# Im2col on one core: eight channels per partition, loads of growing size, first stores of three planes

## The chip, the core and the metric

The kernel runs on one core of a Trainium2 chip. The metric is the device time in microseconds, the median of several runs. Five engines matter by name: VectorE (DVE in the profile) and ScalarE (ACT) copy data inside SBUF, SyncE (SP) issues the transfers, GpSimd (POOL) and TensorE (PE) do no work here. Sixteen DMA engines move the data between HBM and SBUF.

## The reference

The input `x` has 16 batches of 64 channels of 32x32 float32. For each channel, each of the nine offsets of a 3x3 window gives one plane of 30x30 values, cut from the channel at that offset. The output has 16 x 576 planes of 900 values. It is data movement only: 4.19 MB read, 33.18 MB written, no arithmetic.

```python
cols = np.zeros((batch, c * kernel_size * kernel_size, h_out * w_out), dtype=np.float32)
for b in range(batch):
    col_idx = 0
    for i in range(h_out):
        for j in range(w_out):
            patch = x[b, :, i:i + kernel_size, j:j + kernel_size].copy()
            cols[b, :, col_idx] = patch.ravel()
            col_idx += 1
```

## The kernel before, in words

`_im2col_fast` runs with two channels per partition (`CPP` is 2, the first candidate that fits). The 16 x 64 channels make 512 pairs, which are 4 groups of 128 partitions. All four loads are issued first (L32), on SyncE's queue: each brings 128 rows of 8 KB (two channels), 1 MB in all, into an `in_tile` of its own.

Then, for each group, an `out_tile` of 2 x 9 planes per partition (64,800 bytes) is filled by 18 copies of 128x900. Even copies go to ScalarE (L50), odd ones to VectorE (L52), so each engine gets nine. A copy reads a 30x30 window from rows of 32 and writes 900 values in a row. There are two buffers for `out_tile`: the third group's copies must wait until the first group's stores have landed, and the fourth group's for the second's.

Group 0 is stored in two halves, one channel each (L56, 128 rows of 32,400 bytes); groups 1 to 3 are stored in one transfer each (L62, 128 rows of 64,800 bytes). The output of one group is one contiguous stretch of HBM. All loads and stores are issued by SyncE in the order of the program, on one queue. No order is written by hand beyond that; semaphores follow from the tiles' reads and writes.

Of the kernel before, what the change touches and what calls it, by code (L numbers as in the profile page):

```python
# [1 line left out]

# [4 lines left out]


def _im2col_fast(ctx, tc, x, K, out, CPP):  # L10
    nc = tc.nc
    P = nc.NUM_PARTITIONS

    B, C, H, W = x.shape
    HO = H - K + 1
    WO = W - K + 1
    KK = K * K

    ROWS = B * C // CPP
    n_groups = ROWS // P  # L20

    x_v = x.rearrange("b (cp c2) h w -> (b cp) c2 (h w)", c2=CPP)
    out_v = out.rearrange("b (cp c2 kk) n -> (b cp) c2 (kk n)", c2=CPP, kk=KK)

    in_pool = ctx.enter_context(tc.tile_pool(name="in_pool", bufs=n_groups))
    out_pool = ctx.enter_context(tc.tile_pool(name="out_pool", bufs=2))

    in_tiles = []
    for g in range(n_groups):
        row0 = g * P  # L30
        in_tile = in_pool.tile([P, CPP, H, W], x.dtype, name="in_tile")
        nc.sync.dma_start(  # L32
            out=in_tile,
            in_=x_v[row0 : row0 + P].rearrange("r c2 (h w) -> r c2 h w", h=H),
        )
        in_tiles.append(in_tile)

    for g in range(n_groups):
        row0 = g * P
        in_tile = in_tiles[g]  # L40
        out_tile = out_pool.tile([P, CPP, KK, HO, WO], x.dtype)

        ncopy = 0
        for c2 in range(CPP):
            for kk in range(KK):
                ki, kj = divmod(kk, K)
                src = in_tile[:, c2, ki : ki + HO, kj : kj + WO]
                dst = out_tile[:, c2, kk]
                if ncopy % 2 == 0:
                    nc.scalar.copy(out=dst, in_=src)  # L50
                else:
                    nc.vector.tensor_copy(out=dst, in_=src)  # L52
                ncopy += 1

            if g == 0:
                nc.sync.dma_start(  # L56
                    out=out_v[row0 : row0 + P, c2],
                    in_=out_tile[:, c2].rearrange("p kk i j -> p (kk i j)"),
                )

        if g != 0:
            nc.sync.dma_start(  # L62
                out=out_v[row0 : row0 + P].rearrange("r c2 n -> r (c2 n)"),
                in_=out_tile.rearrange("p c2 kk i j -> p (c2 kk i j)"),
            )


def _im2col_generic(ctx, tc, x, K, out):
    nc = tc.nc
    P = nc.NUM_PARTITIONS  # L70

    B, C, H, W = x.shape
    HO = H - K + 1
    WO = W - K + 1
    KK = K * K

    x_rows = x.rearrange("b c h w -> (b c) (h w)")
    out_rows = out.rearrange("b ck n -> (b ck) n").rearrange(
        "(bc kk) n -> bc (kk n)", kk=KK
    )  # L80

    n_rows = B * C
    n_groups = (n_rows + P - 1) // P

    in_pool = ctx.enter_context(tc.tile_pool(name="in_pool", bufs=min(n_groups, 4)))
    out_pool = ctx.enter_context(tc.tile_pool(name="out_pool", bufs=2))

    for g in range(n_groups):
        row0 = g * P
        nrows = min(P, n_rows - row0)  # L90

        in_tile = in_pool.tile([P, H, W], x.dtype, name="in_tile_g")
        nc.sync.dma_start(
            out=in_tile[:nrows],
            in_=x_rows[row0 : row0 + nrows].rearrange("r (h w) -> r h w", h=H),
        )

        out_tile = out_pool.tile([P, KK, HO, WO], x.dtype, name="out_tile_g")
        for kk in range(KK):
            ki, kj = divmod(kk, K)  # L100
            src = in_tile[:nrows, ki : ki + HO, kj : kj + WO]
            dst = out_tile[:nrows, kk]
            if kk % 2 == 0:
                nc.scalar.copy(out=dst, in_=src)
            else:
                nc.vector.tensor_copy(out=dst, in_=src)

        nc.sync.dma_start(
            out=out_rows[row0 : row0 + nrows],
            in_=out_tile[:nrows].rearrange("p kk i j -> p (kk i j)"),  # L110
        )


@with_exitstack
def kernel(
    ctx: ExitStack,
    tc: tile.TileContext,
    x: bass.AP,
    kernel_size: bass.AP,
    out: bass.AP,  # L120
):
    nc = tc.nc
    P = nc.NUM_PARTITIONS

    K = int(kernel_size)
    B, C, H, W = x.shape
    HO = H - K + 1
    WO = W - K + 1
    KK = K * K
    assert out.shape == (B, C * K * K, HO * WO)  # L130

    dt_size = mybir.dt.size(x.dtype)

    CPP = 0
    for cand in (2, 1):
        if C % cand:
            continue
        rows = B * C // cand
        if rows % P:
            continue  # L140
        free_bytes = cand * KK * HO * WO * dt_size
        if free_bytes >= 2**16:
            continue
        n_groups = rows // P
        sbuf_need = 2 * free_bytes + n_groups * cand * H * W * dt_size
        if sbuf_need > 190 * 1024:
            continue
        CPP = cand
        break

    if CPP:
        _im2col_fast(ctx, tc, x, K, out, CPP)
    else:
        _im2col_generic(ctx, tc, x, K, out)


# [1 line left out]
_INS = ['x', 'kernel_size']  # L158
_OUTS = [((16, 576, 900), 'float32')]
#: Inputs that are plain numbers.  # L160
_NUMBERS = {'kernel_size': 3}


# [26 lines left out]
```

## Time and profile before

| | us |
|---|---|
| median of 3 runs | 92.85 (92.7 to 93.08) |
| span of the profiled execution | 91.3 |
| DVE busy, 36 copies | 19.6 |
| ACT busy, 36 copies and a table load | 32.0 |
| mean of a copy, ACT / DVE | 0.938 / 0.623 |
| first load issued / first copies start | 0.73 / 5.61 |

The span is the time from the first to the last instruction of one profiled execution. The runs are timed apart from it, and their median is 1.5 us above it; the profiled execution has no timed value of its own. Over the span the core moved 37.37 MB, a mean of 409 GB/s. A load took a median of 7.9 us from its issue to its landing, the two half stores 16.6 us, the three full stores 30.5 us.

The profile's slices divide the span into 40 equal pieces; a digit is the busy share in tenths. "DMA" in the tables by stage is the mean busy share of the 16 DMA engines. A packet is one row of a transfer, moved by one of them; the trace has the start, length and size of each packet.

### The profile page before, as it was taken

What the parts mean: (1) busy time and instruction counts of PE and PEld (TensorE: products, weight loads), DVE (VectorE), ACT (ScalarE), POOL (GpSimd) and SP (SyncE); (2) the same over time, 40 slices, a digit from 0 to 9 for tenths busy, and PEclk for the clock granted to TensorE, in tenths of its full rate; (3) what the DMA queues carried; (4) which work ended last, traced back from release to release, by engine and by line L of the source; (5) the groups of instructions that cost most, each with busy time, mean ns of one, the idle gap of its engine ahead of it and who ended that gap; (6) DMA issues with size and microseconds to landing.
All of it is one profiled execution on the core that took longest, in us unless ns stands there. A gap on an engine that the chain in (4) does not pass through costs nothing.

```text
span 91.3 us, 141 instructions
## 1 busy us (share of the span) xinstructions
DVE 19.6 (22%) x36; ACT 32.0 (35%) x37; POOL 0.2 (0%) x4
## 2 busy tenths in 40 slices
DVE  0059997000000049600000199000000000000000
ACT  5059999991000049980000199920000000000000
POOL 0000000000000000000000000000000000000000
DMA  2899999999999999899999999999999999999960
GB/s 36 373 406 431 427 463 426 412 440 440 426 426 440 554 454 398 369 426 398 454 454 454 454 454 454 454 454 454 454 454 426 426 398 398 426 426 426 426 284 0
DMA packets 1297, 37.37 MB, mean 409 GB/s; under 512 B 145, under 2 KB 145, under 8 KB 145
## 3 DMA queue, kind: packets, MB, share of 16 engines
q1 hardware_dynamic: 1296, 37.37, 95.7%
q14 instruction: 1, 0.00, 0.0%
HBM read 4.19 MB, written 33.18 MB: 409 GB/s over the span
## 4 chain that ended last, share of the span: by engine, by line
DMA 40%; ACT 24%; ACTq 1%; issue 0%
DMA out_dram<-out_tile 34%; ACT out_tile L50 24%; DMA in_tile<-in_x_dram 5%; ACTq L185 1%; ACTq L50 0%
## 5 line engine op out<-in xcount | busy, mean ns | idle before, releaser
L50 ACT COPY out_tile<-in_tile 128x900 f32<-128x900 f32 x36 | 30.7, 938 | 27.2 <-DMA out_dram<-out_tile 23.6
L52 DVE COPY out_tile<-in_tile 128x900 f32<-128x900 f32 x36 | 19.6, 623 | 37.6 <-DMA out_dram<-out_tile 31.9
L50 ACT ACT_TABLE_LOAD x1 | 1.3, 1283 | 0.7 <-PEq L171 0.7
L171 POOL MEMSET const-bfloat16-1.0<- 128x1 bf16 x1 | 0.1, 102 | 0.0
L171 POOL MEMSET const-uint8-127<- 128x1 uint8 x1 | 0.1, 102 | 0.0
L171 POOL MEMSET const-float32-0.0<- 128x1 f32 x1 | 0.1, 99 | 0.2 <-issue 0.2
L171 POOL MEMSET const-float32-1.0<- 128x1 f32 x1 | 0.1, 99 | 0.0
## 6 DMA issues: line engine op xcount, KB each, us to landing
out_dram<-out_tile SPq DMA_DIRECT2D x3, 8100.0 KB, 30.5
out_dram<-out_tile SPq DMA_DIRECT2D x2, 4050.0 KB, 16.6
in_tile<-in_x_dram SPq DMA_DIRECT2D x4, 1024.0 KB, 7.9
```

Source lines behind the costliest of these rows:

```text
L50: nc.scalar.copy(out=dst, in_=src)
L52: nc.vector.tensor_copy(out=dst, in_=src)
L171: nc = _bacc.Bacc("TRN2", target_bir_lowering=False, num_devices=1)
L185: with _tile.TileContext(nc) as tc:
```

## The change

Each partition now owns eight consecutive channels: 16 x 64 channels over 128 partitions. The four loads bring channel 0, channel 1, channels 2 and 3, and channels 4 to 7 of every partition: rows of 4, 4, 8 and 16 KB, 32 KB apart in HBM. All four are issued first, on SyncE's queue, into tiles of their own.

The output is built in four tiles of two channels, from the same two buffers as before. Planes are given to the engines in a turn of five: VectorE, ScalarE, VectorE, ScalarE, VectorE. VectorE makes 43 planes, ScalarE 29. Channel 0 is stored in three transfers of three planes (rows of 10,800 bytes), channel 1 in one (32,400 bytes), the later tiles in one each (64,800 bytes). Rows of a store are 259,200 bytes apart in HBM. All stores are on SyncE's queue.

The diff, cut to its core:

```diff
-    x_v = x.rearrange("b (cp c2) h w -> (b cp) c2 (h w)", c2=CPP)
-    out_v = out.rearrange("b (cp c2 kk) n -> (b cp) c2 (kk n)", c2=CPP, kk=KK)
-    for g in range(n_groups):
-        row0 = g * P
-        in_tile = in_pool.tile([P, CPP, H, W], x.dtype, name="in_tile")
-        nc.sync.dma_start(
-            out=in_tile,
-            in_=x_v[row0 : row0 + P].rearrange("r c2 (h w) -> r c2 h w", h=H),
-        )
...
-                if ncopy % 2 == 0:
-                    nc.scalar.copy(out=dst, in_=src)
-                else:
-                    nc.vector.tensor_copy(out=dst, in_=src)
...
+    CPP = B * C // P
+    x_v = x.rearrange("b (cp c2) h w -> (b cp) c2 h w", c2=CPP)
+    out_v = out.rearrange("b (cp c2 kk) n -> (b cp) c2 kk n", c2=CPP, kk=KK)
+    in_pool = ctx.enter_context(tc.tile_pool(name="in_pool", bufs=1))
+    out_pool = ctx.enter_context(tc.tile_pool(name="out_pool", bufs=2))
+    loads = [(0, 1), (1, 2), (2, CPP // 2), (CPP // 2, CPP)]
+    home = {}
+
+    def load(i, queue):
+        c0, c1 = loads[i]
+        t = in_pool.tile([P, c1 - c0, H, W], x.dtype, name=f"in_tile{i}")
+        queue.dma_start(
+            out=t.rearrange("p c h w -> p (c h w)"),
+            in_=x_v[:, c0:c1].rearrange("p c h w -> p (c h w)"),
+        )
+        for c in range(c0, c1):
+            home[c] = (t, c0)
+
+    def plane(dst, c, kk, engine):
+        t, base = home[c]
+        ki, kj = divmod(kk, K)
+        src = t[:, c - base, ki : ki + HO, kj : kj + WO]
+        if engine == 0:
+            nc.vector.tensor_copy(out=dst[:, kk], in_=src)
+        else:
+            nc.scalar.copy(out=dst[:, kk], in_=src)
+
+    def store(c, n, k0, k1, t, slot):
+        if n == 1:
+            nc.sync.dma_start(
+                out=out_v[:, c, k0:k1].rearrange("p kk n -> p (kk n)"),
+                in_=t[:, slot, k0:k1].rearrange("p kk i j -> p (kk i j)"),
+            )
+        else:
+            nc.sync.dma_start(
+                out=out_v[:, c : c + n].rearrange("p c kk n -> p (c kk n)"),
+                in_=t.rearrange("p c kk i j -> p (c kk i j)"),
+            )
+
+    for i in range(len(loads)):
+        load(i, nc.sync)
+
+    turn = (0, 1, 0, 1, 0)
+    n = 0
+    for c in range(0, CPP, 2):
+        out_tile = out_pool.tile([P, 2, KK, HO, WO], x.dtype, name="out_tile")
+        for s in range(2):
+            for kk in range(KK):
+                plane(out_tile[:, s], c + s, kk, turn[n % len(turn)])
+                n += 1
+                if c == 0 and s == 0 and kk % K == K - 1:
+                    store(c, 1, kk + 1 - K, kk + 1, out_tile, 0)
+            if c == 0 and s == 1:
+                store(1, 1, 0, KK, out_tile, 1)
+        if c > 0:
+            store(c, 2, 0, KK, out_tile, 0)
```

More of the change, by code (lines that the diff above doesn't have):

```diff
@@ L5 @@
 import concourse.tile as tile
-from concourse import bass_utils, mybir
+from concourse import mybir
 from concourse._compat import with_exitstack
[L10 to L20, printed above, removed]
-    x_v = x.rearrange("b (cp c2) h w -> (b cp) c2 (h w)", c2=CPP)
-    out_v = out.rearrange("b (cp c2 kk) n -> (b cp) c2 (kk n)", c2=CPP, kk=KK)
-    in_pool = ctx.enter_context(tc.tile_pool(name="in_pool", bufs=n_groups))
-    out_pool = ctx.enter_context(tc.tile_pool(name="out_pool", bufs=2))
-    in_tiles = []
-    for g in range(n_groups):
-        row0 = g * P
-        in_tile = in_pool.tile([P, CPP, H, W], x.dtype, name="in_tile")
-        nc.sync.dma_start(
-            out=in_tile,
-            in_=x_v[row0 : row0 + P].rearrange("r c2 (h w) -> r c2 h w", h=H),
-        )
[L36 to L48, printed above, removed]
-                if ncopy % 2 == 0:
-                    nc.scalar.copy(out=dst, in_=src)
-                else:
[L52 to L65, printed above, removed]
@@ L68, in _im2col_generic @@
[L68 to L111, printed above, removed]
@@ L129 @@
     KK = K * K
[L130 to L154, printed above, removed]
+    assert out.shape == (B, C * KK, HO * WO)
+    CPP = B * C // P
+    assert CPP * P == B * C and C % CPP == 0 and CPP % 4 == 0
+    x_v = x.rearrange("b (cp c2) h w -> (b cp) c2 h w", c2=CPP)
+    out_v = out.rearrange("b (cp c2 kk) n -> (b cp) c2 kk n", c2=CPP, kk=KK)
+    in_pool = ctx.enter_context(tc.tile_pool(name="in_pool", bufs=1))
+    out_pool = ctx.enter_context(tc.tile_pool(name="out_pool", bufs=2))
```

## The prediction

> **What bounds the kernel now.** I read the slices of the page first, then the queue table, the rates by stage, the chain, the waits, and last the single DMA packets that the trace records.
>
> ```profile
> DVE  0059997000000049600000199000000000000000
> ACT  5059999991000049980000199920000000000000
> DMA  2899999999999999899999999999999999999960
> ...
> q1 hardware_dynamic: 1296, 37.37, 95.7%
> ```
>
> Each slice is 2.28 us. The copy engines rest through most of the span; the DMA engines don't, from the second slice to the last but one. The one queue's packets took 95.7% of 16 engines' time, which is 87.4 us of 91.3. So the bound is DMA throughput, and only the two ends of the span and the pace of a packet can move the time.
>
> The rates by stage (us, DVE and ACT busy, clock, DMA share, GB/s) are:
>
> ```profile
> 1.80:5.60 3.80, 0.00 (x0) 0.21 (x1) 0.00 (x0) 1.00 0.86 341
> 5.60:10.00 4.40, 4.39 (x9) 4.39 (x6) 0.00 (x0) 1.00 1.01 426
> ...
> 33.10:52.20 19.10, 4.93 (x9) 7.69 (x9) 0.00 (x0) 1.00 1.00 434
> 52.20:71.30 19.10, 4.93 (x9) 7.69 (x9) 0.00 (x0) 1.00 1.00 434
> ```
>
> Loads run at 426 GB/s, stores of 64,800 B rows at 434. The chain of waits looks as if it named another culprit:
>
> ```profile
> 5.61 15.30 ACT out_tile L50 x18
> 20.90 0.02 issue
> 20.92 31.21 DMA out_dram<-out_tile
> ```
>
> It gives ACT 15.3 us. But the store issued at 20.92 took 31.2 us to land, and its 8.3 MB need only 19.1 at 434 GB/s: it stood some 11 us behind other stores. A faster ACT would only lengthen that queue. The waits say the same from the other side:
>
> ```profile
> DVE out_tile L52 <- DMA out_dram<-out_tile: 31.9, 2, 17.7
> ACT out_tile L50 <- DMA out_dram<-out_tile: 23.6, 2, 12.2
> ```
>
> Both copy engines wait for buffers that stores hold, not the stores for copies.
>
> The packet records give the sum. A packet is one partition's row, and each of the 16 engines takes 8 rows of every transfer. The first packet starts at 1.77 us (the first load is issued at 0.73), the last ends at 89.93, its semaphore arrives at 90.44, the span ends at 91.28. Median times: 8,192 B (load) 309 ns, 32,400 B 1200 ns, 64,800 B 2391 ns. The two stores fix a line: (2391-1200)/32,400 gives 27.2 B/ns, and 9 ns over for each packet; 8,192 B falls on it (301+9). Per engine: loads 32 x 309 = 9.89 us, stores of the first tile 16 x 1200 = 19.20, the others 24 x 2391 = 57.38, nine semaphore writes of 9 ns 0.08: 86.55. The records sum to 87.33 on average. The loads hold most of the rest: 0.44 us in the first packets (up to 1252 ns each, reads starting) and 0.24 in the last four or so of each engine, from 11.2 to 12.7 us, where loads give way to stores. The engines start at different times (1.77 to 2.55 us) and end spread over 1.07 us; they never wait for one another, and the last sets the end.
>
> **What the Trainium skill says.** "DMA: Bandwidth & Descriptors", section "Where 436 GB/s comes from", sets a ceiling of 435 GB/s at the SBUF ports; the trace's stores run at 434, so they have no more to gain. The same page, "Why small descriptors are slow (HBM only)", charges a fixed few cycles for each packet; the trace has 9 ns, which I use. Its section "Queues, rings and completion order" says that an engine takes one ring's descriptors in order. The trace agrees: the first store was issued at 9.96 us and its first packet starts at 12.3, when an engine's load packets are through. Its section "Latency and other measured facts" lists a row pitch of 512 KiB at 207 GB/s per direction against 214 at full rate, and of 4 MiB at 103; no run here shows a pitch of 32 KiB, which the changed loads have.
>
> **The change, part by part.** The sum is made against the profiled span of 91.28 us; the median of the timed runs is 92.85, so 1.57 us lie outside it, and I carry the difference in span over to the median.
>
> First load of one channel. It has 8 packets of 4,096 B per engine, by the line 151+9 = 160 ns each: 1.28 us where 8 of 8,192 B took 2.47. It lands 1.19 us earlier, and the copies start at 4.4 instead of 5.61. Worth nothing by itself: the second load is issued right behind (an issue took 0.77 us the first time, then about 0.4), so it is in the ring at about 2.5 to 3 us, before the first load's packets end at 3.9 or so. If that cover failed, the engines would idle a few tenths.
>
> Loads in all. Four transfers as before, 32 packets per engine as before: 16 x 160 + 8 x 309 + 8 x (602+9) = 9.92 against 9.89. Cost 0.03 us, rounding really. The three later loads' landing moves with them: about 5.7, 8.2 and 13 us.
>
> First stores of three planes. The turn is DVE, ACT, DVE, ACT, DVE, so planes 0 to 2 need two DVE copies and one ACT copy. From start to start a DVE copy took 9.77/18 = 0.54 us and an ACT copy 15.29/18 = 0.85. First store ready at 4.4 + 1.2 = 5.6 instead of 9.96. It can't leave then: on the same ring 4.2 MB of loads stand ahead until 12.3. Gain zero, hidden by the loads. Its price stays: per engine 24 packets of 10,800 B, each 397+9 = 406 ns, 9.75 us, where 8 x 1200 = 9.60 stood. Cost 0.15 us, all on the path. Two more transfers put two more semaphore writes of 9 ns on each engine: 0.02. SP issues two more stores (0.34 us each, beside DMA work): nothing.
>
> Copies shared 3 to 2. DVE gets 43 planes, ACT 29: 43 x 0.54 = 23.3 us, 29 x 0.85 = 24.6, where ACT had 36 x 0.85 = 30.6. The first tile is done near 10.5 us, the second near 16.5 (was 20.9), and its store isn't due until 32. Later tiles take about 6 us from the release of their buffer at 33.1 and 52.2, where ACT took 7.7; their turn on the ring comes at 52 and 71. A wait of 12 us on the ring becomes 13. Zero, off the path. The third tile's copies now wait for four stores and the last load; these end together in ring order, at the time two stores did before, plus 0.17.
>
> Eight channels per partition. Rows read lie 32 KiB apart, in pieces of 4, 4, 8 and 16 KiB; rows written 259,200 B apart instead of touching. Same bytes, same packet sizes for the big stores. The bounds: below, nothing to gain beyond the losses named above; above, the 512 KiB entry is 3% of 10 us, 0.3, and the 4 MiB entry would double the loads, +10 us. I take zero, since the pitch is sixteen times below the lightest entry and 259,200 is no power of two.
>
> Tail. The last store is the same 8.3 MB with nothing beside it: unchanged. Total 0.03 + 0.15 + 0.02 = 0.2 us on the path: span 91.5, median **93.0**.
>
> **Rivals.**
>
> *A queued store slows the loads ahead of it* (slower). The slow load packets appear at 11.2 us, about a microsecond after the first store is issued. Either the engines look a few packets ahead (then the cost stays 0.24 us), or a store in the ring slows every load packet from then on. In the slow stretch packets took 309 to 418 ns, means of 342 and 378 in its first two half microseconds, so some 18% of the time is lost. With the store in the ring from about 6.8 us, that holds for 5.5 us until 12.3: 1.0 us instead of 0.24, +0.8: 93.8. Against it: the stretch also begins just where each engine has about four packets left. It decides if load packets are slow before 10 us.
>
> *The new addresses are slower* (slower). Loads at the 3% of the 512 KiB entry and stores at 1% of 76.6 us add 0.3 + 0.8, to about 94.1; one of the two gives 93.3 to 93.8. For it: some engines took 2414 ns for stores instead of 2391, so HBM isn't always free of effect. Against it: nearly all packets run at the port's rate.
>
> *The ends shrink* (faster). Smaller first packets fill the engines sooner, and the handover and the spread at the end get smaller. These hold 0.44 + 0.24 us and about 0.6 between the mean and the last engine's end; half of it is 0.6: 92.4. Against it: start latency doesn't depend on size in anything shown.
>
> *The change does not do what it says.* It would be that the early stores never start early; I hold that for certain on one ring, and it is part of the forecast.
>
> **How the numbers follow.** Forecast 0.58, with its own range of 92.5 to 93.4 (the spread of the engines' ends moves by some tenths). Queued store 0.20, addresses 0.12, ends shrink 0.10. Faster or slower by over 0.5%, 0.46 us, is about what a measurement of this kernel can tell from no change: faster 0.10, same 0.58, slower 0.32. The range takes in most of the first two rivals: 92.4 to 94.0.
>
> **What would show it.** Copies from about 4.4 us; the first store issued near 5.7 but taking 10 us and more to land; ACT's COPY group x29 near 27 us busy, DVE's x43; DMA slices still at 9 throughout; packets of 160, 406, 611 and 2391 ns; the last packet near 90.1. Wrong if load packets are slow from 7 us on, if large stores depart from 2391 ns, or if a gap opens between the first loads.

## The result and the profile after

The changed kernel takes 93.88 us (median of 4 runs) beside 92.89 for the kernel before on the same chip: a ratio of 1.0095, 95% interval 1.0073 to 1.0117, which is 0.88 us. (One of the four runs, 95.58 us, was disturbed and isn't in the ratio.) It is slower, by about 1%, and clear of noise. The profiled execution took 93.83 us, its span is 92.0 us where before it was 91.3.

The page of the changed kernel, the copy engines' and DMA slices and the queue:

```profile
DVE  0199999000000039900000099600000000000000
ACT  5199999000000039960000099500000000000000
...
DMA  2999979999999999999999999999999787999990
GB/s 44 372 438 456 356 246 418 432 437 446 432 451 451 451 451 451 451 451 451 451 451 451 451 451 451 451 451 451 451 451 422 338 366 338 422 394 422 451 451 0
...
q1 hardware_dynamic: 1584, 37.37, 96.3%
```

The DMA engines are as busy as before, 96.3% of the span; there is no gap to find. But busy isn't moving: in the fifth and sixth slices, 9.2 to 13.8 us (counting the slices from zero), the rate drops to 356 and 246 GB/s. Those are the last loads. The kernel before has no such dip there:

```profile
GB/s 36 373 406 431 427 463 426 412 440 440 426 426 440 554 454 398 369 426 398 454 454 454 454 454 454 454 454 454 454 454 426 426 398 398 426 426 426 426 284 0
```

The rates by stage of the changed kernel show the same, and that the big stores run as they did (a line has the window, its length, the busy time of DVE, ACT and POOL, the clock, the DMA share and GB/s):

```profile
5.60:10.00 4.40, 4.40 (x9) 4.40 (x6) 0.00 (x0) 1.00 1.06 447
10.00:12.40 2.40, 2.40 (x6) 2.40 (x4) 0.00 (x0) 1.00 0.98 246
...
33.10:52.20 19.10, 5.47 (x10) 6.85 (x8) 0.00 (x0) 1.00 1.00 434
```

The second of these windows read, before the change:

```profile
10.00:12.40 2.40, 2.40 (x6) 2.40 (x4) 0.00 (x0) 1.00 1.07 416
```

Between 10 and 12.4 us the engines of the changed kernel are 98% busy and begin packets at only 246 GB/s. (Share and rate count a whole packet in the window where it starts, so a share can exceed 1, and the dip is a little sharper than the truth.) The timeline of the changed kernel places it against the stores:

```profile
4.28 11.92 ACT L58 COPY out_tile<-in_tile 128x900 f32<-128x900 f32 x14 [2.27 <-DMA in_tile<-in_x_dram]
4.28 11.92 DVE L56 COPY out_tile<-in_tile 128x900 f32<-128x900 f32 x22 [4.28 <-DMA in_tile<-in_x_dram]
5.54 5.15 SPq L62 DMA_DIRECT2D out_dram<-out_tile  x4
16.27 43.04 SPq L67 DMA_DIRECT2D out_dram<-out_tile  x3
```

The copies start 1.3 us earlier than before, the first store is issued 4.4 us earlier, the second tile's store 4.6 us earlier. None of it comes out at the end.

The packet records, summed as in the prediction (us per engine; "excess" is the time above the usual length of a load packet of that size, 159, 309 or 611 ns for rows of 4, 8 or 16 KB):

| | before | after |
|---|---|---|
| all packets | 87.33 | 88.63 |
| excess in the first load packets, to 6 us | 0.44 | 0.48 |
| excess in the later load packets | 0.24 | 1.24 |
| mean of a 10,800 B packet, ns | - | 406.2 |
| median of a 64,800 B packet, ns | 2391 | 2398 |
| last engine's end after the mean engine's | 0.56 | 0.27 |

Of the 1.30 us that the packets grew, 1.00 is in the later load packets, all of it in the 16 KB rows. On every engine the first four or more of its eight take exactly 611 ns; the last two to four are slower, up to 1276 ns. That is the whole of the slowdown and more; the engines ending closer together gives 0.29 back, and about 0.36 us less passes before and between the packets, so that the last packet ends 0.65 us later (90.57 us where it was 89.92).

The chain of waits of the changed kernel again names a copy engine, and again it isn't the bound:

```profile
4.28 11.93 DVE out_tile L56 x22
16.21 0.02 SPq L67
16.24 0.03 issue
16.27 36.52 DMA out_dram<-out_tile
```

The store issued at 16.27 took 36.5 us to land: the 4.6 us that the copies gained turned into a longer stay in the queue.

### The profile page after: what moved, and what is told of

The parts are those of the page before. It is cut to its first block, busy times and chain, and to the rows that moved or that the text cites. A ratio compares the mean times of both kernels' runs of the same rounds, so it can differ in the third digit from the quotient of the medians.

```text
span 92.0 us, 145 instructions
## 1 busy us (share of the span) xinstructions
DVE 23.4 (25%) x43; ACT 26.1 (28%) x30; POOL 0.2 (0%) x4
## 3 DMA queue, kind: packets, MB, share of 16 engines
q1 hardware_dynamic: 1584, 37.37, 96.3%
## 4 chain that ended last, share of the span: by engine, by line
DMA 44%; DVE 19%; DVEq 1%; issue 0%; SPq 0%
DMA out_dram<-out_tile 40%; DVE out_tile L56 19%; DMA in_tile<-in_x_dram 4%; DVEq L120 1%; DVEq L56 0%; SPq L67 0%
## 5 line engine op out<-in xcount | busy, mean ns | idle before, releaser
L58 ACT COPY out_tile<-in_tile 128x900 f32<-128x900 f32 x29 | 24.8, 938 | 32.1 <-DMA out_dram<-out_tile 29.8
L56 DVE COPY out_tile<-in_tile 128x900 f32<-128x900 f32 x43 | 23.4, 625 | 35.5 <-DMA out_dram<-out_tile 31.2
## 6 DMA issues: line engine op xcount, KB each, us to landing
out_dram<-out_tile SPq DMA_DIRECT2D x1, 4050.0 KB, 23.3
in_tile<-in_x_dram SPq DMA_DIRECT2D x1, 2048.0 KB, 12.1
```

The lines of the kernel that those rows point to most:

```text
L56: nc.vector.tensor_copy(out=dst[:, kk], in_=src)
L58: nc.scalar.copy(out=dst[:, kk], in_=src)
```

## The experiments

Four theories could explain the slow packets. **S**: the last four load packets of each engine suffer from the stores behind them, and bigger packets suffer more. **Q**: what matters is how early the stores are in the ring. **N**: the many small stores do it. **G**: the new addresses do it. In every run below, "late loss" is the excess of the load packets after 6 us, 0.24 us before and 1.24 after; it comes from one profiled execution of each kernel. A ratio compares a kernel with the kernel before as it was measured beside it (92.69 to 92.89 us); differences of ratios are given in points, a point being 1%.

### The packet size of the last loads

Two kernels change only the loads of the changed kernel.

```diff
-    loads = [(0, 1), (1, 2), (2, CPP // 2), (CPP // 2, CPP)]
+    loads = [(0, 1), (1, 2), (2, 4), (4, 6), (6, 8)]
```

> The changed kernel with its last load (rows of 16 KB) cut into two of 8 KB rows, nothing else. Theory S (the last four load packets of each engine are slowed by the stores that stand behind them, and the loss grows with the size of those packets): loss in the load packets falls from 1.24 us to about 0.25 as in the kernel before, packets are slow only from about 11 us, time about 92.9. Theory Q (the loss comes from how early the stores are in the ring, whatever the packets' size): the loss stays near 1 us, time about 93.7.

It took 94.09 us, ratio 1.0147 (1.0117 to 1.0177). Late loss 0.93 us: the 8 KB packets are slow from 10.3 us on. The ratio is 0.5 points above the changed kernel's although the loss is smaller; the two intervals meet, and nothing here explains the rest.

```diff
-    loads = [(0, 1), (1, 2), (2, CPP // 2), (CPP // 2, CPP)]
+    loads = [(0, 1), (1, 5), (5, 7), (7, 8)]
```

> The changed kernel's four load sizes in another order: rows of 4, 16, 8 and 4 KB, so that the last load has 4 KB rows; same packets, same stores. Theory S: the 16 KB packets all take 611 ns, only the last four 4 KB packets are slowed, loss under 0.2 us, time about 92.8. Theory Q: loss near 1 us again, time about 93.7. A theory that 16 KB rows are slow by themselves: they are slow here too, 93.7.

It took 93.85 us, ratio 1.0116 (1.0091 to 1.014). The 16 KB packets, now in the middle, take 615 ns on average; the 8 and 4 KB packets behind them carry a late loss of 1.15 us. S falls in both runs, and so does the idea that 16 KB rows are slow by themselves. It isn't the last four packets that are slow but the last stretch of the loads, whatever its packets: when the third slow packet of the main group starts, about 46 to 63 KB per engine of loads are left in these runs, in the changed kernel and in the next one, near 2 us at full rate.

### One store for channel 0

```diff
-                if c == 0 and s == 0 and kk % K == K - 1:
-                    store(c, 1, kk + 1 - K, kk + 1, out_tile, 0)
+                if c == 0 and s == 0 and kk == KK - 1:
+                    store(c, 1, 0, KK, out_tile, 0)
```

> The changed kernel with channel 0 stored in one transfer of 32,400 B rows, not three of 10,800 B. Theory S: load packets keep their loss of about 1.2 us, only 16 packets of overhead and two semaphore writes per engine go, -0.17 us: about 93.6. Rival N (the many small store packets behind the loads cause the loss): it falls to about 0.25 us, time about 92.7.

It took 93.41 us, ratio 1.0065 (1.0041 to 1.009). The first store is issued at 7.93 us and the late loss is 0.96 us. N falls as the main cause. The gain over the changed kernel, 0.3 points, isn't clear of noise, as the two intervals overlap; 0.17 us of small packets and a loss lower by 0.28 us would make it 0.45 us.

### No store behind the loads

The pairs of channels are worked in falling order, so that the first store needs the last load.

```diff
-    for c in range(0, CPP, 2):
+    for c in range(CPP - 2, -1, -2):
...
-                if c == 0 and s == 0 and kk % K == K - 1:
+                if c == CPP - 2 and s == 0 and kk % K == K - 1:
...
-            if c == 0 and s == 1:
-                store(1, 1, 0, KK, out_tile, 1)
-        if c > 0:
+            if c == CPP - 2 and s == 1:
+                store(c + 1, 1, 0, KK, out_tile, 1)
+        if c < CPP - 2:
```

> The changed kernel with the channels worked in falling order of pairs (6 and 7 first), so that no store can be in the ring before the last load has landed. Theories S, Q and N: every 16 KB packet takes 611 ns, loss zero in the loads, but the ring stands empty from the end of the loads, about 12.2 us, until about 15: time about 95 to 96. If 16 KB load packets are slow at the end by themselves (by the copies at work or by the memory): the last four are slow here too.

A single run took 95.57 us. Every 16 KB packet takes 611 ns, late loss zero. Its slices show the price, the hole from 12.8 to 15.3 us while the first planes are copied:

```profile
DVE  0000039999600009940000079800000000000000
...
DMA  3999915999999999999988778999999999999990
GB/s 40 353 438 468 433 56 221 442 428 392 507 442 442 442 663 442 442 442 442 442 387 387 304 304 387 442 442 442 442 442 442 442 442 442 442 442 442 442 442 0
```

So without a store behind the loads there is no loss. The copies aren't running in this kernel while the loads end, though, so this run alone doesn't exclude them as the cause; the runs with a late store below do.

### The time of the first store

```diff
-                if c == 0 and s == 0 and kk % K == K - 1:
-                    store(c, 1, kk + 1 - K, kk + 1, out_tile, 0)
-            if c == 0 and s == 1:
-                store(1, 1, 0, KK, out_tile, 1)
-        if c > 0:
-            store(c, 2, 0, KK, out_tile, 0)
+        store(c, 2, 0, KK, out_tile, 0)
```

> The changed kernel with the first tile stored in one transfer like the others, so that the first store is issued near 10.8 us, 1.5 us before the loads end, and not at 5.54. Theory L (a store that is already in the ring slows the load packets of about the last 50 KB of each engine, some 2.5 us; one that comes later slows fewer): the loss in the load packets is at most 0.25 us, and 0.3 us of small packets and semaphore writes goes too: about 92.6. Rival G (the new addresses, eight channels per partition, cost it): loss stays near 1 us, about 93.5.

It took 92.21 us, ratio 0.9942 (0.9926 to 0.9958): faster than both kernels. Late loss zero. Its timeline:

```profile
0.73 1.81 SPq L44 DMA_DIRECT2D in_tile<-in_x_dram  x4
...
10.48 47.35 SPq L67 DMA_DIRECT2D out_dram<-out_tile  x4
```

That kernel changes the time of the first store and the number of stores at once. The next one changes only when the first tile's stores are issued. Nothing but the order of the first tile's copies differs from the changed kernel: the planes that complete the small stores come last.

```diff
-        for s in range(2):
-            for kk in range(KK):
-                plane(out_tile[:, s], c + s, kk, turn[n % len(turn)])
-                n += 1
-                if c == 0 and s == 0 and kk % K == K - 1:
-                    store(c, 1, kk + 1 - K, kk + 1, out_tile, 0)
-            if c == 0 and s == 1:
-                store(1, 1, 0, KK, out_tile, 1)
+        todo = [(s, kk) for s in range(2) for kk in range(KK)]
+        if c == 0:
+            last = [(0, 2), (0, 5), (0, 8)]
+            todo = [t for t in todo if t not in last] + last
+        for s, kk in todo:
+            plane(out_tile[:, s], c + s, kk, turn[n % len(turn)])
+            n += 1
+            if c == 0 and (s, kk) in last:
+                store(c, 1, kk + 1 - K, kk + 1, out_tile, 0)
+        if c == 0:
+            store(1, 1, 0, KK, out_tile, 1)
```

> The changed kernel with the same loads and the same four stores of the first tile, on the same queue in the same order; only planes 2, 5 and 8 of channel 0 are copied last in the tile, so that the first small store is issued near 10 us and not at 5.54. Theory L (it is the time at which the first store stands in the ring): the loss in the load packets falls from 1.24 us to at most 0.3; small packets and semaphore writes, 0.17 us, stay: about 92.4. Rival N (small stores themselves cause it): loss near 1 us, about 93.5.

It took 92.73 us, ratio 1.0004 (0.9994 to 1.0015), with 13 runs. Late loss zero. The timeline and the rate of the last stretch of loads in this kernel:

```profile
4.57 11.92 ACT L58 COPY out_tile<-in_tile 128x900 f32<-128x900 f32 x14 [2.56 <-DMA in_tile<-in_x_dram]
4.57 11.92 DVE L56 COPY out_tile<-in_tile 128x900 f32<-128x900 f32 x22 [4.57 <-DMA in_tile<-in_x_dram]
10.12 3.31 SPq L62 DMA_DIRECT2D out_dram<-out_tile  x4
```

```profile
9.00:11.00 2.00, 2.00 (x4) 2.00 (x3) 0.00 (x0) 1.00 1.03 442
11.00:13.00 2.00, 2.00 (x5) 2.00 (x3) 0.00 (x0) 1.00 0.96 410
```

The same windows of the changed kernel read:

```profile
9.00:11.00 2.00, 2.00 (x5) 2.00 (x3) 0.00 (x0) 1.00 1.05 360
11.00:13.00 2.00, 2.00 (x5) 2.00 (x4) 0.00 (x0) 1.00 1.00 254
```

Same loads, same stores in the same order, same copies at the same pace beside them. The three small stores are issued at 10.12, 10.60 and 10.99 us here, at 5.54, 6.60 and 7.79 in the changed kernel, and the store of channel 1 at 12.18 where it was 10.36. Issuing them later takes the loss away, and with it 0.91 points of the ratio, 0.84 us, some 0.24 points either way. That the stores are issued so early is the cause, and the copies aren't part of it.

### Each half of the change on the kernel before

The addresses alone, eight channels per partition:

```diff
-    x_v = x.rearrange("b (cp c2) h w -> (b cp) c2 (h w)", c2=CPP)
-    out_v = out.rearrange("b (cp c2 kk) n -> (b cp) c2 (kk n)", c2=CPP, kk=KK)
+    x_v = x.rearrange("b (cp c8) h w -> (b cp) c8 (h w)", c8=8)
+    out_v = out.rearrange("b (cp c8 kk) n -> (b cp) c8 (kk n)", c8=8, kk=KK)
...
-            in_=x_v[row0 : row0 + P].rearrange("r c2 (h w) -> r c2 h w", h=H),
+            in_=x_v[:, CPP * g : CPP * g + CPP].rearrange("r c2 (h w) -> r c2 h w", h=H),
...
-                    out=out_v[row0 : row0 + P, c2],
+                    out=out_v[:, CPP * g + c2],
...
-                out=out_v[row0 : row0 + P].rearrange("r c2 n -> r (c2 n)"),
+                out=out_v[:, CPP * g : CPP * g + CPP].rearrange("r c2 n -> r (c2 n)"),
```

> The kernel before with only the addresses changed: eight consecutive channels per partition, four loads of two channels (8 KB rows 32 KB apart), stores of the same shapes 259,200 bytes apart, same copies and order. Theory L: no difference, 92.8, loss in the loads about 0.25 us. Rival G: about 93.5.

It took 92.45 us, ratio 0.9966 (0.9954 to 0.9979): a little faster than before, which neither theory expected. Late loss 0.19 us, big store packets a median of 2391 ns as before; what differs is the end, where the last engine comes 0.19 us after the mean one, not 0.56. G falls.

The early small stores alone:

```diff
-            if g == 0:
+                if g == 0 and c2 == 0 and kk % K == K - 1:
+                    n0 = (kk + 1 - K) * HO * WO
+                    n1 = (kk + 1) * HO * WO
+                    nc.sync.dma_start(
+                        out=out_v[row0 : row0 + P, c2, n0:n1],
+                        in_=out_tile[:, c2, kk + 1 - K : kk + 1].rearrange("p kk i j -> p (kk i j)"),
+                    )
+
+            if g == 0 and c2 == 1:
```

> The kernel before with one part of the change alone: channel 0 of the first group stored in three transfers of three planes, the first issued near 7.5 us and not at 9.96. Theory L: the loss in the 8 KB load packets rises from 0.24 to about 0.9 us and small packets add 0.17: about 93.6. Rival G: only the 0.17 is added, about 93.0.

It took 94.0 us, ratio 1.0133 (1.0116 to 1.015). The first store is issued at 7.39 us, the late loss is 0.95 us. The kernel before gets the fault of the changed one from this part alone. The windows of this kernel, with the 8 KB packets and the old addresses, show the dip too:

```profile
9.00:11.00 2.00, 2.00 (x5) 2.00 (x4) 0.00 (x0) 1.00 0.98 397
11.00:13.00 2.00, 2.00 (x5) 2.00 (x3) 0.00 (x0) 1.00 0.94 242
```

### Does the slow stretch move with the end of the loads?

```diff
     for i in range(len(loads)):
         load(i, nc.sync)
+    extra = in_pool.tile([P, 2, H, W], x.dtype, name="extra")
+    nc.sync.dma_start(
+        out=extra.rearrange("p c h w -> p (c h w)"),
+        in_=x_v[:, 6:8].rearrange("p c h w -> p (c h w)"),
+    )
```

> The changed kernel with a fifth load of 1 MB (channels 6 and 7 again, 8 KB rows) whose data nothing uses, behind the other four: 2.5 us more of loads in front of the same stores. Theory L: the slow load packets move with the end of the loads, from 9.5 us to about 12, the 16 KB packets stay at 611 ns for the most part. Rival E (an event near 10 us, such as the copies' end or the issue of the fourth store, slows them): packets are slow from 9.5 to 10 us on again, and for longer, up to 14.5. Time 96.2 by L, up to 97 by E.

A single run took 96.45 us. The 16 KB packets take 611 ns, though the first store stands in the ring as early as in the changed kernel (issued at 5.70 us); the fifth load's packets carry a late loss of 1.13 us, from 12.4 us on. Windows of this kernel:

```profile
9.00:11.00 2.00, 2.00 (x5) 2.00 (x3) 0.00 (x0) 1.00 1.05 451
11.00:13.00 2.00, 2.00 (x4) 2.00 (x4) 0.00 (x0) 1.00 0.96 381
13.00:15.00 2.00, 2.00 (x5) 2.00 (x3) 0.00 (x0) 1.00 0.96 225
```

The stretch of slow packets is tied to the end of the loads, and so to the place of the stores behind them, not to an event near 10 us. A store far behind in the ring does no harm here; it does once the loads ahead of it are down to the last 2 to 3 us.

### The early stores on another queue

```diff
         if n == 1:
-            nc.sync.dma_start(
+            nc.scalar.dma_start(
```

> The changed kernel with the four stores of the first tile issued by ScalarE on its own queue, as early as before; loads and later stores stay on SyncE's. If the loss comes from stores standing behind loads in one ring: the stores start near 7 us between the loads, and the loss is gone or small, about 92.6. If it comes from reads and writes of HBM going on at once in the DMA engines, whatever the ring: load packets are slow from 7 us until the loads end, near 20 us, and the time is 94 or more. The issues cost ScalarE some 0.35 us each, beside other work.

It took 101.53 us, ratio 1.096 (1.0943 to 1.0976), but from another cause, as its waits show:

```profile
DVE out_tile L56 <- DMA out_dram<-out_tile: 36.1, 1, 36.1
ACT out_tile L58 <- DMA out_dram<-out_tile: 35.1, 1, 35.1
```

The store of channel 1, on its own queue, shared the engines with the second tile's store on the other one and took 40.8 us to land; both buffers came free only at 52.4 us, and the DMA engines then stood empty for some 8 us. On the question asked it is half an answer: late loss 0.65 us, 0.56 of it between 7.1 and 10 us. The first store packet starts only at 9.69 us, though its store was issued at 5.68: most of the slow load packets come before any store packet has begun, and with 5 us of loads still to go. Once loads and stores run side by side, from 10 us to the end of the loads near 15, the loss is 0.09 us. Neither forecast holds: the loss doesn't vanish with a ring of its own, and reads beside writes aren't slow for as long as they last. What this kernel shares with the others is that the load packets are slow shortly before the first store packets start, which on one ring is the end of the loads.

## Why the prediction was right or wrong

The measured 93.88 us lies within the outer range of 92.4 to 94.0, but outside the forecast's own 92.5 to 93.4, and the forecast of no clear change, held at 0.58, missed a slowdown of 0.95%. The outer range held because it took in the first rival, held at 0.20; it wasn't the forecast's mechanism that earned it.

- **The bound** was right: DMA throughput from end to end. The copies' earlier start, the 3 to 2 sharing and the shorter tiles brought nothing, as forecast; ACT's 29 copies took 24.8 us busy, DVE's 43 took 23.4. (The forecast had 24.6 and 23.3 in its sum; the "near 27" among its signs is 29 times the length of one copy, 0.938 us, which counts the overlap of neighbouring copies twice.)
- **Small packets**: 24 per engine of 406.2 ns, as worked out; with two more semaphore writes 0.17 us on the path. The large stores stayed near 2391 ns: a mean of 2397.0 where it was 2394.3, 0.07 us in all.
- **Loads in all, "cost 0.03 us"**, is the step that failed. It priced the packets at their full rate and carried the 0.24 us at the handover from loads to stores over as a constant. It was 1.24: the term was too small by 1.00 us, and the run with the same stores issued late shows what was missing from it: the early stores behind the loads. The step "first stores" made the same slip from the other side: it asked whether the early store gains anything and found that the loads hide it, and gave its presence in the ring no price.
- **The first rival** had the right place: a store queued behind the loads slows them. By its own test, load packets slow before 10 us, it came true, with the first slow one at 9.51 us. Its mechanism, every load packet from then on, was wrong: the first four 16 KB packets per engine ran at 611 ns with the store in the ring. It was a short stretch at the end, but one in time or bytes, not the "four packets" of the other reading, as the runs with 8 and 4 KB rows showed. That its price, +0.8 us, came near the +1.00 measured is partly luck: too long a stretch at too small a loss per packet. Its reading of the stretch was also off: the slow packets before took up to 646 ns, not 418, and means of 342 and 378 against 309 lose some 14% of the time, not 18, which would have made it +0.5. The kernel before was spared by its late first store (9.96 us), not by its packet size.

Late loss against the issue of the first store, in kernels with the same loads in bytes and all on one queue: issued at 10.48 and 10.12 us, 0; at 9.96 and 9.79, 0.24 and 0.19; at 7.93 and 7.39, 0.96 and 0.95; at 5.71, 5.54 and 5.48, 0.93, 1.24 and 1.15. So the loss grows steeply between 10 and 8 us and little, if at all, for stores that are earlier still.

- **Addresses** were taken at zero. The Trainium skill, "DMA: Bandwidth & Descriptors", section "Latency and other measured facts", gave no entry for a 32 KiB pitch; here such loads ran at full rate (8 KB packets a median of 309 ns), and the layout alone measured a ratio of 0.9966, a small gain.
- **The sum**, in points of the ratio: layout -0.34 (its own run); the same stores issued late 0.04, so that small stores and the other parts together take about 0.38 back (a remainder, not measured by itself); early instead of late +0.91. Together 0.95, each term with an uncertainty of 0.1 to 0.25. The forecast of 93.0 had the 0.17 us and missed the last.

What stays open is what in a DMA engine makes the last loads slow. That it reads ahead into the store is a guess. It fits a stretch of fixed length, and it fits the run with two queues, where load packets were slow before any store packet had begun; but no record shows the reads and writes of a packet apart.

## What to carry to other kernels

With the DMA engines busy from end to end, making data ready earlier bought nothing here, and stores put early behind loads in the same ring cost 0.84 us for 4.6 us of earliness. In a kernel of this kind it is worth trying to issue the first store so that it arrives shortly before the loads end, in as few transfers as that allows; one store of the whole first tile, issued at 10.48 us with the engines' last load packets ending from 12.1 to 12.5, gave 92.21 us, the best of all kernels tried. And a DMA share of 98% says only that packets are in flight: read it together with the GB/s, and the single packets against their usual length.

## What the hardware showed that was not expected

- A store that has long been in the ring slows the load packets of about the last 46 to 63 KB of each engine to as much as two or three times their length (611 to 1276 ns at 16 KB, 309 to 900 at 8 KB), whatever their size, for about 1 us lost in all. Issued 1.9 and 2.2 us before the loads end on the mean engine (10.48 and 10.12 us), it cost nothing.
- With the stores on another queue, load packets were slow from 7.08 us, 2.6 us before the first store packet started.
- The engines end more evenly with eight channels per partition in the layout run (0.19 us from mean to last, 0.56 before), about as much as that run gained. The other kernel with the old addresses had 0.48, the others with the new ones 0.10 to 0.43, each in one execution; that the addresses do it isn't shown, and why was not tried.
- Three transfers of 10,800 B rows and one of 32,400 instead of one of 64,800 cost 0.52 us between the two kernels with a late first store (92.73 and 92.21; 0.62 points of the ratio), of which packet sums explain 0.35 and the spread at the end 0.20.
